# A hybrid encoder layer on one core: negated maximum inside the score pass, value halves read from PSUM, and four moves of work between queues

## The chip, the cores and the metric

The kernel runs on one core of a Trainium2 chip. The metric is the device time of one execution in microseconds (us). A core has five engines with an instruction queue each: TensorE (PE; its weight loads are listed apart as PEld), VectorE (DVE), ScalarE (ACT), GpSimd (POOL) and SyncE (SP, which only issues DMAs). DMAs are issued from SP's or GpSimd's queue. Each queue runs in order; an instruction that waits holds up all that stand behind it on its engine.

## The reference

One layer of an encoder over 4096 positions of width 1024, all in float32. A normed input goes through one wide projection, whose columns feed two groups. Group A is a bidirectional mLSTM with a chunkwise scan (32 chunks of 128, 4 heads of 128). Group B is windowed attention: 8 query heads on 2 key heads of 64, a window of 128 to either side, a relative-position bias and a sink logit per head. The outputs of both go through one output projection, the residual is added and a last norm taken. The part that the change touches most:

```python
scores = jnp.where(mask[None, :, None, None], scores + bias, NEG_INF)
sink_l = sink.astype(jnp.float32).reshape(B_KV_HEADS, Q_PER_KV)[:, :, None]
m = jnp.maximum(jnp.max(scores, axis=-1), sink_l)
p = jnp.exp(scores - m[..., None])
denom = jnp.sum(p, axis=-1) + jnp.exp(sink_l - m)
out = jnp.einsum('bnhgqk,bnkhd->bnqhgd', p, vw) / denom.transpose(0, 1, 4, 2, 3)[..., None]
```

## The kernel before

float32 products are made of three passes of a shorter format: each operand is split into a high half (a cast, on ACT) and a low half (the difference, on DVE), and high·low, low·high and high·high are added up in PSUM. So nearly every result of TensorE is followed by a pair: a cast on ACT and a subtraction on DVE behind it. PE's order is written out by hand: the program walks lists of "pieces" (work with dependencies) and spreads them over a list of "fill" (projection matmuls), and PE runs in exactly that order. The orders on the other engines are set by a scheduler, which takes what is ready, earlier work of the program first; `tc.high_priority` moves a group ahead, and `behind(c, x)` keeps a group from being issued ahead of the instruction x.

There are four stages, by the times of the profile: attention (0 to 607 us), projections of group A with its chunk sums (607 to 1205), the scan (1205 to 1700), and the output side (1700 to the end).

**Attention.** A slot `sl` is one block n of 128 queries and one key head (kv = sl % 2); there are 64. For each of a slot's four groups g (two heads by two halves of the queries), `att_a` multiplies queries with up to 320 keys into a PSUM tile `sp`; L383, one pass of DVE, adds the bias table G and writes s to SBUF, and its accumulator takes the row maximum into a column of `st`. After the fourth group L390 makes NG = min(−maximum, −sink) for all four columns at once, and four exps (L392, ACT) of s + NG follow. `att_t` transposes the exps in three groups of four (`tp`, PSUM tag "b", two buffers), L414 casts them and L415 makes the low half, which frees the buffer. `att_o` multiplies with the values into `op` (PSUM tag "c", one buffer); L438 and L439 (`ab`) read it out. `slot` mixes scores of slot sl + 2, transposes of sl and products of sl − 1. In between run the projections of later blocks: queries (`qp`; L559 and L563 split them), keys (`kk`, L496 to L502) and values (`vp`), and `norm_rows`, which squares two rows of blocks on ACT (L213, 1024 columns each). In steady state two blocks of queries (four slots) make a period of some 35 us. The values: L523 copies the second half of `vp` to `vg`, L524 adds the first, L527 casts and L528 subtracts, the last two from `vg` in SBUF. At the stage's end `sinks` adds the sinks' share, and `rnorm` (L800) takes the reciprocal of all denominators R, which is transposed and stored later.

**Projections.** Blocks of 512 positions from b = 7 down to 0. For each of 8 row groups m, matmuls with `xb` (loaded by L868 on SP; block 7's comes from the attention) give U; L1051 to L1058 apply the convolution and the activation, and L1060 stores the result to `q_d` (m < 4) or `k_d`. `weigh(n)` forms the weighted values of a chunk (`wvr` L1112, `wvh` L1114, `wvl` L1115); `ktp` transposes the keys (L1099), and L1101 and L1102 split them into `kt`; `kvp` multiplies the two into a state `kv`.

**Scan.** For a chunk n, `load` brings E (decay rows, 2 × 256 KB), W, q, k, v and others; GpSimd masks E (L1442), ACT takes its exponentials (L1446), DVE multiplies with the scores S (L1456), and `heads` uses the result. `pieces` of a chunk are spread over its share of the output side's matmuls (`P`, with operands `op` from L1239).

The call that orders a chunk of the scan, since the change turns on it:

```python
with behind(c, c.rawd if n == 0 else None):
    load(n + 2, ("e",))
    if n == 0:
        load(2, ("q",))
```

Of the kernel before, what the change touches and what calls it, by code (L numbers as in the profile page):

```python
# [9 lines left out]
F32 = mybir.dt.float32  # L10
# [3 lines left out]
ALU = mybir.AluOpType  # L14
# [14 lines left out]
def f32(ap):  # L29
    return ap.bitcast(F32)  # L30
# [85 lines left out]
def behind(c, ins):  # L116
    return c.tc.issue_after(ins.ins) if ins is not None else ExitStack()
# [43 lines left out]
def pass1(c):  # L161
    nc, tc, A = c.nc, c.tc, c.A
    NB = 16
    with ExitStack() as es:
# [196 lines left out]
        def att_a(sl, g):  # L361
# [10 lines left out]
            if g == 0:  # L372
                st = wk.tile([128, 4], F32, tag="st", bufs=4, name=f"st{sl}")
                ST[sl] = ([], list(range(jl // 128, jr // 128)), st)
            ps, _, mx = ST[sl]
            ng, rs = c.NG[:, kv, n, :], c.R[:, n, kv, :]
            sp = c.ps("a", [128, 384], f"sp{sl}_{g}")
            qt = qb[kv * 2 + m][:, qc // 64 + half].rearrange("p z q -> p (z q)")
            for z in range(2):
# [4 lines left out]
                                           in1=bias[0][:, kv * 2 + m, lo - 64 * half:hi - 64 * half],  # L384
                                           op0=ALU.add, op1=ALU.max, scale=1.0, scalar=-3e38,
                                           accum_out=mx[:, g:g + 1])
            ps.append(s)
            if g < 3:
                return
            nc.vector.scalar_tensor_tensor(ng, mx, -1.0, nsink[:, kv].rearrange("p h m -> p (h m)"), ALU.mult, ALU.min)  # L390
            for g in range(4):
                LAST["act"] = nc.scalar.activation(ps[g][:, kept(g)], ps[g][:, kept(g)], AF.Exp, bias=ng[:, g:g + 1],  # L392
                                                   accum_out=rs[:, g:g + 1])
# [11 lines left out]
        def att_t(sl, i):  # L405
            ps, js, _ = ST[sl]
            if i >= len(js):
# [98 lines left out]
        def vproj(b):  # L506
            R = {}

            def unit(i, k):
# [12 lines left out]
                with tc.high_priority(offset=EV):  # L522
                    nc.scalar.copy(vg, vp[:, 1, :])  # L523
                    nc.vector.tensor_add(vg, vp[:, 0, :], vg)  # L524
                vt = wk.tile([128, 2, 128], F32R, tag="v", bufs=7, name=f"v{n}")
                vv = vg[:, 0:128].rearrange("p (a d) -> p a d", a=2)
                nc.scalar.copy(vt[:, :, 0:64], vv)  # L527
                nc.vector.tensor_sub(vt[:, :, 64:128], vv, f32(vt[:, :, 0:64]))  # L528
                V[n] = vt
# [153 lines left out]
        fill = qproj(NB - 2) + kproj(NB - 1) + vproj(NB - 1) + qproj(NB - 1) + v2_units(range(31, 27, -1))  # L683
        interleave(fill, pieces)
        sinks()

# [111 lines left out]
def rnorm(c):  # L798
    nc = c.nc
    nc.vector.reciprocal(c.R, c.R)  # L800
    tp = c.ps("b", [128, 2, 128], "rtp")
# [76 lines left out]
def pass2(c):  # L878
    nc, tc, A = c.nc, c.tc, c.A
    with ExitStack() as es:  # L880
# [138 lines left out]
        def qkproj(b, m):  # L1019
# [6 lines left out]
            def unit(lo, hi, k, j):  # L1026
# [28 lines left out]
                def finish():  # L1055
# [3 lines left out]
                    dst = c.k_d if m >= 4 else c.q_d  # L1059
                    nc.sync.dma_start(dst[4 * b:4 * b + 4, :, h * 128:h * 128 + 128].rearrange("n p t -> p n t"),  # L1060
                                      acc.rearrange("p (n t) -> p n t", n=4))
# [83 lines left out]
        for b in range(7, -1, -1):  # L1145
# [40 lines left out]
            def kvp(n, hh):  # L1186
                if hh == 0 and n > n3 - 3:
                    weigh(n - 1)
                kvmm(n, hh)
# [226 lines left out]
def pass3(c):  # L1416
    nc, tc, A = c.nc, c.tc, c.A
    with ExitStack() as es:
# [9 lines left out]
        def load(n, names):  # L1428
            load_scan(c, n, names)
# [111 lines left out]
        for n in range(NCH):  # L1541
# [3 lines left out]
            if m < NCH:  # L1545
                with behind(c, c.em):
                    state(n)
            with behind(c, c.rawd if n == 0 else None):
                load(n + 2, ("e",))
                if n == 0:  # L1550
                    load(2, ("q",))
            fill = take(c, 42)
# [8 lines left out]
            pieces += [(lambda h=h: heads(n, h)) for h in range(NH)]  # L1561
            pieces.insert(4, lambda: load(m, ("v",)) if n else None)
            pieces.append(lambda: (load(n + 2, ("kf",)), weigh_q(m) if m > 1 else None))
            if n:
# [360 lines left out]
```

## Time and profile before

| what | value |
|---|---|
| time, median of 3 runs | 2175.59 us (2173.66 to 2176.89) |
| the profiled execution | 2170.39 us, its span 2168.7 us |
| granted clock of TensorE in it | 0.999 |
| busy: PE, DVE, ACT, POOL | 2116.4, 1547.1, 1132.2, 704.2 us |
| DMA | 460.71 MB, 212 GB/s on average |

The rows of the profile name a line of the kernel (L383), an engine, an operation, and the tiles that it writes and reads (`s<-sp,G`). Times are us from the start of the span, and durations of single instructions in ns where the column says so. "Idle before, releaser" is the time that an engine stood still ahead of a group, and what ended it. SPq is SP's queue, on which a row is the issue of a DMA. PEclk of 1.0 is TensorE at full clock.

### The profile page before, as it was taken

How to read it: one execution, taken by the hardware profiler on the slowest of the kernel's cores; microseconds unless marked ns; L12 is line 12 of the kernel's file. 1: busy time of each engine (PE TensorE's matmuls, PEld its weight loads, DVE VectorE, ACT ScalarE, POOL GpSimd, SP SyncE). 2: the span in 40 equal slices, each digit the busy share in tenths (PEclk: the TensorE clock that was granted, in tenths of full speed). 3: DMA queues.
4: the chain of work that ended last, by engine and by line, in shares of the span. 5: the costliest groups of instructions: out<-in, count | busy, mean ns of one | idle time of the engine just before them, and what ended most of it. 6: DMA issues, size and time to landing. Idle time of an engine off the chain costs nothing. (4 is left out here: it accounts for less than half of the span.)

```text
span 2168.7 us, 35317 instructions
## 1 busy us (share of the span) xinstructions
PE 2116.4 (98%) x12034; PEld 1834.4 (85%) x12034; DVE 1547.1 (71%) x3259; ACT 1132.2 (52%) x2764; POOL 704.2 (32%) x1049
## 2 busy tenths in 40 slices
PE   8999999999999999999999999999999999999998
PEld 7999999999887887888887888888888788888886
DVE  6777777878876786667566777777777443777776
ACT  7778777778654444444433455555555321323323
POOL 3575666653014234322310322223222111112222
PEclk9999999999999999999999999999999999999999
DMA  8563544433228556743676988888888998667775
GB/s 269 181 208 135 194 142 187 161 139 113 64 91 263 188 170 217 246 159 112 216 223 239 340 272 273 254 265 278 268 273 290 353 359 279 181 178 187 192 196 144
DMA packets 286432, 460.71 MB, mean 212 GB/s; under 512 B 23851, under 2 KB 151851, under 8 KB 284716
## 3 DMA queue, kind: packets, MB, share of 16 engines
q1 hardware_dynamic: 246880, 323.94, 46.5%
q0 software_dynamic: 39136, 134.25, 19.0%
q8 instruction: 95, 1.56, 0.3%
q14 instruction: 85, 0.70, 0.1%
q10 hardware_dynamic: 236, 0.27, 0.0%
HBM read 305.20 MB, written 153.17 MB: 211 GB/s over the span
## 5 line engine op out<-in xcount | busy, mean ns | idle before, releaser
L1342 PE MATMUL P<-wt,op 128*128 128x512 f32 x1344 | 360.4, 406 | 0.4 <-DMA op<-xT_d 0.4
L1034 PE MATMUL up<-xb,w 128*128 128x512 f32 x1344 | 335.0, 396 | 0.0
L1691 PE MATMUL o<-wo,yo 128*128 128x512 f32 (+1 forms) x1356 | 311.7, 392 | 0.0
L1691 PEld LDWEIGHTS o<-wo,yo 128*128 128x128 f32 x1356 | 253.2, 188 | 58.6
L1034 PEld LDWEIGHTS up<-xb,w 128*128 128x128 f32 x1344 | 245.1, 188 | 49.1
L1342 PEld LDWEIGHTS P<-wt,op 128*128 128x128 f32 x1344 | 238.5, 189 | 42.5 <-DMA op<-xT_d 0.8
L1053 DVE SCALAR_TENSOR_TENSOR qk<-U,cw,qk 128x512 f32<-128x512 f32 x256 | 194.0, 760 | 85.2 <-ACT qk L1051 81.7
L549 PE MATMUL qp<-xT,wqb 128*128 128x256 f32 x1536 | 241.5, 287 | 0.1
L549 PEld LDWEIGHTS qp<-xT,wqb 128*128 128x128 f32 x1536 | 213.2, 189 | 8.6 <-DVE wqb L320 0.5
L392 ACT ACTIVATE s<-s,NG 128x320 f32<-128x320 f32 (+1 forms) x256 | 140.2, 550 | 46.9 <-DVE NG L390 46.3
L1007 PE MATMUL v2p<-w,xb 128*128 128x512 f32 x672 | 159.1, 396 | 4.7 <-DMA xb<-xT_d 3.1
L1007 PEld LDWEIGHTS v2p<-w,xb 128*128 128x128 f32 x672 | 125.7, 188 | 36.8 <-DMA xb<-xT_d 4.0
L415 DVE TENSOR_TENSOR pt<-tp,pt 128x512 fp32r<-128x512 f32 x188 | 127.9, 687 | 34.1 <-ACT pt L414 32.8
L383 DVE CUSTOM_DVE_ANT_0 s<-sp,G 128x320 f32<-128x320 f32 (+1 forms) x256 | 122.3, 478 | 27.8 <-PE sp L380 25.8
L414 ACT CAST pt<-tp 128x512 fp32r<-128x512 f32 x188 | 108.6, 585 | 52.0 <-PE tp L412 40.3
L412 PE MATMUL tp<-ident,s 128*128 128x128 f32 x752 | 113.5, 273 | 15.9 <-DVE pt L415 15.6
L426 PE MATMUL op<-pt,v 128*128 128x512 f32 x376 | 120.5, 401 | 7.0 <-DVE ab L439 7.0
L380 PE MATMUL sp<-kk,q 128*128 128x320 f32 (+2 forms) x512 | 118.6, 312 | 1.3 <-DVE kk L502 0.8
L1493 ACT ACTIVATE hs<-num,r 128x128 f32<-128x128 f32 x128 | 46.7, 365 | 129.7 <-DVE r L1490 70.9
L151 PE MATMUL zbp<-xc,w 128*128 128x512 f32 x256 | 102.2, 399 | 1.9 <-DVE az L1405 1.4
L412 PEld LDWEIGHTS tp<-ident,s 128*128 128x128 f32 x752 | 85.5, 140 | 20.8 <-issue 17.7
L153 PE MATMUL zbp<-xc,w 128*128 128x512 f32 x256 | 101.0, 395 | 0.0
(307 smaller groups left out, 4543.2 us busy)
## 6 DMA issues: line engine op xcount, KB each, us to landing
xc<-xT_d SPq DMA_DIRECT2D x64, 512.0 KB, 7.3
xT_d<-xT POOLq DMA_DIRECT2D x52, 512.0 KB, 7.3
xb<-xT_d SPq DMA_DIRECT2D x48, 514.0 KB, 7.1
op<-xT_d SPq DMA_DIRECT2D x96, 256.0 KB, 5.5
E<-m_d SPq DMA_DIRECT2D x64, 256.0 KB, 4.3
W<-w_d SPq DMA_DIRECT2D x64, 256.0 KB, 5.9
y<-y_d SPq DMA_DIRECT2D x32, 512.0 KB, 3.4
out<-xr POOLq DMA_DIRECT2D x31, 512.0 KB, 4.4
```

The lines of the kernel that those rows point to most:

```text
L380: nc.tensor.matmul(sp[:, lo:hi], qt, kk[:, kv, z, col - 128 + lo:col - 128 + hi], start=(z == 0), stop=(z == 1))
L383: nc.vector.tensor_tensor_reduce(out=s[:, lo:hi], in0=sp[:, lo:hi], in1=bias[0][:, kv * 2 + m, lo - 64 * half:hi - 64 * half], op0=ALU.add ...
L392: LAST["act"] = nc.scalar.activation(ps[g][:, kept(g)], ps[g][:, kept(g)], AF.Exp, bias=ng[:, g:g + 1], accum_out=rs[:, g:g + 1])
L412: nc.tensor.transpose(tp[:, g * 128:(g + 1) * 128], ps[g][:, j * 128:(j + 1) * 128], c.ident)
L415: nc.vector.tensor_sub(pt[:, 1, :], tp, f32(pt[:, 0, :]))
L426: nc.tensor.matmul(op, vt, pt[:, z, :], start=(i == 0 and z == 0), stop=(i == len(js) - 1 and z == 1))
L549: nc.tensor.matmul(qp, wq[k // 2][:, k % 2, w, m * 128:m * 128 + 128], x[k], start=(k == 0 and j == 0), stop=(k == KT - 1 and j == 2))
L1007: nc.tensor.matmul(vp, a, wv[k // 2][:, k % 2, m, :], start=(k == 0 and j == 0), stop=(k == KT - 1 and j == 2))
L1034: nc.tensor.matmul(up[:, 0:hi - lo], w[k // 2][:, k % 2, a, cs], x, start=(k == 0 and j == 0), stop=(k == KT - 1 and j == 2))
L1053: nc.vector.scalar_tensor_tensor(acc, U[:, t:t + 512], cw[:, cm, t:t + 1], acc, ALU.mult, ALU.add)
L1342: nc.tensor.matmul(P[i], OPS[j, i][:, k, z, :], c.wt[i][k][m], start=k == 0 and a == 0, stop=k == 3 and a == 2)
L1691: nc.tensor.matmul(p, a[:, z, k, :], w[k // 2][:, k % 2, m, lo:hi], start=k == 0 and z == 1, stop=k == 3 and z == 0 and m == 0)
```

## The change

- L383 computes −(score + bias) and takes the minimum, starting from −sink, which it reads from a column of SBUF (`nsink`); the result goes to NG itself. L390 and the tile `st` are gone. s is stored negated, and the exps have a scale of −1.
- The sum of the two halves of `vp` is made by two adds, one of 128 columns (for b > 2 in place in PSUM) and one of 16 columns (to `vg`, the gates). For b > 2 the cast and the subtraction read the sum from PSUM, and stand in a high-priority group.
- The reciprocal in `rnorm` is issued behind the last L439 of the attention.
- The stores of `q_d` of block 7 are issued from GpSimd's queue in place of SP's.
- At block 0 of the projections the last three `weigh` are issued behind the `kt` pair that was last written by then.
- In the scan, E for chunk n + 2 is loaded as a piece of its own behind the first group of heads, instead of at the chunk's start (for n > 0), so that most chunks have 12 pieces where there were 11.

```diff
-                st = wk.tile([128, 4], F32, tag="st", bufs=4, name=f"st{sl}")
-                ST[sl] = ([], list(range(jl // 128, jr // 128)), st)
-            ps, _, mx = ST[sl]
+                ST[sl] = ([], list(range(jl // 128, jr // 128)))
+            ps, _ = ST[sl]
...
-                                           op0=ALU.add, op1=ALU.max, scale=1.0, scalar=-3e38,
-                                           accum_out=mx[:, g:g + 1])
+                                           op0=ALU.add, op1=ALU.min, scale=-1.0,
+                                           scalar=nsink[:, kv, half, m:m + 1], accum_out=ng[:, g:g + 1])
...
-            nc.vector.scalar_tensor_tensor(ng, mx, -1.0, nsink[:, kv].rearrange("p h m -> p (h m)"), ALU.mult, ALU.min)
             for g in range(4):
-                LAST["act"] = nc.scalar.activation(ps[g][:, kept(g)], ps[g][:, kept(g)], AF.Exp, bias=ng[:, g:g + 1],
+                LAST["act"] = nc.scalar.activation(ps[g][:, kept(g)], ps[g][:, kept(g)], AF.Exp, scale=-1.0, bias=ng[:, g:g + 1],
...
-                    nc.vector.tensor_add(vg, vp[:, 0, :], vg)
+                    for o, cs in ((vp[:, 0, 0:128] if b > 2 else vg[:, 0:128], slice(0, 128)), (vg[:, 128:144], slice(128, 144))):
+                        nc.vector.tensor_add(o, vp[:, 0, cs], vg[:, cs])
                 vt = wk.tile([128, 2, 128], F32R, tag="v", bufs=7, name=f"v{n}")
-                vv = vg[:, 0:128].rearrange("p (a d) -> p a d", a=2)
-                nc.scalar.copy(vt[:, :, 0:64], vv)
-                nc.vector.tensor_sub(vt[:, :, 64:128], vv, f32(vt[:, :, 0:64]))
+                vv = (vp[:, 0, 0:128] if b > 2 else vg[:, 0:128]).rearrange("p (a d) -> p a d", a=2)
+                with tc.high_priority(offset=EV if b > 2 else 0):
+                    nc.scalar.copy(vt[:, :, 0:64], vv)
+                    nc.vector.tensor_sub(vt[:, :, 64:128], vv, f32(vt[:, :, 0:64]))
...
         interleave(fill, pieces)
+        c.abv = LAST["abv"]
         sinks()
...
-    nc.vector.reciprocal(c.R, c.R)
+    with behind(c, c.abv):
+        nc.vector.reciprocal(c.R, c.R)
...
-                    nc.sync.dma_start(dst[4 * b:4 * b + 4, :, h * 128:h * 128 + 128].rearrange("n p t -> p n t"),
+                    q = nc.gpsimd if b == 7 and m < 4 else nc.sync
+                    q.dma_start(dst[4 * b:4 * b + 4, :, h * 128:h * 128 + 128].rearrange("n p t -> p n t"),
...
-                    weigh(n - 1)
+                    with behind(c, None if b else c.kta), behind(c, None if b else c.ktv):
+                        weigh(n - 1)
...
-            with behind(c, c.rawd if n == 0 else None):
-                load(n + 2, ("e",))
-                if n == 0:
-                    load(2, ("q",))
+            if n == 0:
+                with behind(c, c.rawd):
+                    load(2, ("e", "q"))
...
+            if n:
+                pieces.insert(3, lambda: load(n + 2, ("e",)))
```

The change also moves instructions on ACT, DVE, GpSimd and SP, since the scheduler sets their order. In the rows below a name carries two numbers, the program's own and a running one; the changed kernel's lines are 2 to 4 numbers off.

ACT in a steady period, around the squares `jk8`, before. `s0_` and `s1_` are score tiles of which a slot uses two and two, `pt16_2` the third transposed group of slot 16, whose cast frees the buffer that a group of slot 17 takes:

```order
L414 CAST pt16_1_2655<-tp16_1_2650 128x512
L392 ACTIVATE s0_0_136,R_95<-s0_0_136,NG_160 128x320
L392 ACTIVATE s0_1_137,R_95<-s0_1_137,NG_160 128x320
L559 ACTIVATE q5_1_2712<-qp5_1_2647 64x4x64 x2
L392 ACTIVATE s1_0_142,R_95<-s1_0_142,NG_160 128x320
L392 ACTIVATE s1_1_143,R_95<-s1_1_143,NG_160 128x320
L213 ACTIVATE jk8_0_2698,ss8_2697<-xr8_2588 128x1024
L213 ACTIVATE jk8_1_2700,ss8_2697<-xr8_2588 128x1024
L414 CAST pt16_2_2690<-tp16_2_2685 128x512
```

The same place after the change:

```order
L390 ACTIVATE s1_0_142,R_95<-s1_0_142,NG_160 128x320
L436 COPY ab7_2522<-op15_2576 64x2x4x64
L412 CAST pt16_1_2630<-tp16_1_2625 128x512
L390 ACTIVATE s1_1_143,R_95<-s1_1_143,NG_160 128x320
L213 ACTIVATE jk8_0_2672,ss8_2671<-xr8_2564 128x1024
L213 ACTIVATE jk8_1_2674,ss8_2671<-xr8_2564 128x1024
L559 ACTIVATE q5_1_2686<-qp5_1_2622 64x4x64 x2
L390 ACTIVATE s0_2_138,R_95<-s0_2_138,NG_160 128x320
L412 CAST pt16_2_2664<-tp16_2_2659 128x512
```

Between the casts of `pt16_1` and `pt16_2` stood all four exps of a slot and two squares; now there stand the last exp of that slot, the squares, and the first exp of the next slot.

DVE at the end of the projections, before (`kt0_h` are the key halves of block 0's four heads, `wvr`/`wvl` the weighted values of chunks 1 and 0):

```order
L1115 TENSOR_TENSOR wvl1_13491<-wvr1_13492,wvh1_13490 128x1032
L1112 TENSOR_TENSOR wvr0_13545<-v2_0_13002,TM_8490 128x4x129
L1053 SCALAR_TENSOR_TENSOR qk0_7_13324<-U0_7_13296,cw_7445,qk0_7_13324 128x512
L1058 SCALAR_TENSOR_TENSOR qk0_6_13286<-th0_6_13330,qk0_6_13286 128x512
L1102 TENSOR_TENSOR kt0_0_1_13367<-ktp0_0_13361,kt0_0_0_13366 128x512
L1102 TENSOR_TENSOR kt0_1_1_13387<-ktp0_1_13381,kt0_1_0_13386 128x512
L1053 SCALAR_TENSOR_TENSOR qk0_7_13324<-U0_7_13296,cw_7445,qk0_7_13324 128x512
L1115 TENSOR_TENSOR wvl0_13544<-wvr0_13545,wvh0_13543 128x1032
```

The same place after the change:

```order
L1105 TENSOR_TENSOR kt0_0_1_13271<-ktp0_0_13265,kt0_0_0_13270 128x512
L1055 SCALAR_TENSOR_TENSOR qk0_7_13228<-U0_7_13200,cw_7358,qk0_7_13228 128x512 x2
L1105 TENSOR_TENSOR kt0_1_1_13291<-ktp0_1_13285,kt0_1_0_13290 128x512
L1327 TENSOR_TENSOR o1_13306<-P0_1_13280,o0_13278 128x512
L1060 SCALAR_TENSOR_TENSOR qk0_7_13228<-th0_7_13295,qk0_7_13228 128x512
L1105 TENSOR_TENSOR kt0_2_1_13319<-ktp0_2_13313,kt0_2_0_13318 128x512
L1115 TENSOR_TENSOR wvr2_13330<-v2_2_12844,TM_8394 128x4x129
L1140 SCALAR_TENSOR_TENSOR C3_13336<-C4_12716,decay_8208,kv3_0_13338 128x129
L1329 TENSOR_TENSOR z0_13346<-P0_2_13308,o1_13306 128x512
L1118 TENSOR_TENSOR wvl2_13329<-wvr2_13330,wvh2_13328 128x1032
```

The weighting of chunks 2, 1 and 0 stood ahead of the four `kt` copies or between them; that of chunk 2 now stands behind the third copy, and the other two further on.

SP at the first loads of `xb` for block 6, before:

```order
L807 DMA r_d_80<-rt_8338 128x128 x2
L1060 DMA k_d_75<-qk7_6_8279 128x4x128
L1060 DMA k_d_75<-qk7_7_8397 128x4x128
L1060 DMA q_d_74<-qk7_0_8484 128x4x128
L868 DMA xb6_0_8664<-xT_d_69 128x2x514
L868 DMA xb6_1_8666<-xT_d_69 128x2x514
```

The same place after the change:

```order
L809 DMA r_d_80<-rt_8242 128x128 x2
L1063 DMA k_d_75<-qk7_6_8183 128x4x128
L1063 DMA k_d_75<-qk7_7_8301 128x4x128
L870 DMA xb6_0_8568<-xT_d_69 128x2x514
L870 DMA xb6_1_8570<-xT_d_69 128x2x514
```

The store of the first q rows of block 7 no longer stands ahead of the loads; it is in GpSimd's queue.

More of the change, by code (lines that the diff above doesn't have):

```diff
@@ L405, in att_t @@
         def att_t(sl, i):
-            ps, js, _ = ST[sl]
+            ps, js = ST[sl]
             if i >= len(js):
```

## Prediction

> **What bounds the kernel now.** I read the page first: the busy shares, then the chain.
>
> ```profile
> span 2168.7 us, 35317 instructions
> PE 2116.4 (98%) x12034; PEld 1834.4 (85%) x12034; DVE 1547.1 (71%) x3259; ACT 1132.2 (52%) x2764; POOL 704.2 (32%) x1049
> ```
>
> TensorE is busy for 2116.4 of 2168.7 us. The change leaves its instructions and their order alone up to the scan, and their number everywhere, so what can be won is the 2168.7 − 2116.4 = 52.3 us in which it idles. The next view is therefore the waits of PE (engine and line, what it waited for: us in total, times, longest):
>
> ```profile
> PE tp L412 <- DVE pt L415: 15.6, 13, 1.8
> PE op L426 <- DVE ab L439: 7.0, 6, 2.4
> PE bps L337 <- POOL ohb L300: 6.5, 1, 6.5
> PE v2p L1007 <- DMA xb<-xT_d: 3.1, 2, 2.1
> PE ktp L1099 <- DVE kt L1102: 2.8, 2, 1.5
> ```
>
> The edits touch four of these five. The 6.5 us at the start (bias table) stay. Restricted to 110 to 560 us, the first row reads 14.3 us in 10 waits: one of about 1.4 us in each period of some 35 us, the attention's steady state. The fence has that row and the next, then the busy time of PE, PEld, DVE, ACT and POOL in one such period, and then one of the waits, by the timelines of ACT, DVE and PE (start, duration, and in brackets the idle time before it and what ended it):
>
> ```profile
> PE tp L412 <- DVE pt L415: 14.3, 10, 1.8
> PE op L426 <- DVE ab L439: 1.0, 2, 0.7
> ...
> 228.00:263.00 35.00, 33.59 (x256) 32.35 (x255) 27.04 (x70) 27.21 (x72) 21.86 (x29) 1.00 0.46 162
> ...
> 231.38 0.56 ACT L392 ACTIVATE s<-s,NG 128x320 f32<-128x320 f32 x1 [2.20 <-DVE NG L390]
> ...
> 232.48 0.75 ACT L559 ACTIVATE q<-qp 64x256 fp32r<-64x256 f32 x2
> ...
> 234.37 1.04 ACT L213 ACTIVATE jk<-xr 128x1024 bf16<-128x1024 f32 x1
> 235.41 1.04 ACT L213 ACTIVATE jk<-xr 128x1024 bf16<-128x1024 f32 x1
> 236.57 1.07 ACT L414 CAST pt<-tp 128x512 fp32r<-128x512 f32 x2
> ...
> 229.32 0.49 DVE L383 CUSTOM_DVE_ANT_0 s<-sp,G 128x320 f32<-128x320 f32 x1
> ...
> 230.34 1.00 DVE L390 SCALAR_TENSOR_TENSOR NG<-st,nsink 128x4 f32<-128x4 f32 x1
> ...
> 237.19 1.29 DVE L415 TENSOR_TENSOR pt<-tp,pt 128x512 fp32r<-128x512 f32 x2
> ...
> 238.03 0.63 PE L412 MATMUL tp<-ident,s 128*128 128x128 f32 x4 [1.41 <-DVE pt L415]
> ```
>
> Read backwards: the transposes at 238.03 need a PSUM buffer which L415 frees at 237.88; L415 needs the cast L414, which at 236.57 is the first thing on ACT after four exps, two query copies and two squares L213. All four exps waited until 231.38 for L390, the four-column bias instruction, and ACT stood idle for 2.20 us before them. PE would have been ready at 238.03 − 1.41 = 236.62.
>
> **The negated maximum (64 times L390 out).** The pass L383 now yields the negated, sink-limited maximum, so an exp waits for its own L383 and not for the fourth. These are the groups of DVE up to 660 us (count, busy us, mean ns) and, below them, single lines (ns minimum, median, maximum):
>
> ```profile
> L390 DVE SCALAR_TENSOR_TENSOR NG<-st,nsink 128x4 f32<-128x4 f32 x64 | 42.2, 659 | 1.0
> L528 DVE TENSOR_TENSOR v<-vg,v 128x128 fp32r<-128x128 f32 x32 | 21.1, 661 | 0.1
> L524 DVE TENSOR_TENSOR vg<-vp,vg 128x144 f32<-128x144 f32 x32 | 9.4, 298 | 0.0
> ...
> L390 DVE SCALAR_TENSOR_TENSOR NG<-st,nsink x64: 143/164/1839, 39.6 to 592.8; 128x4 f32<-128x4 f32 x64
> ...
> L383 DVE CUSTOM_DVE_ANT_0 s<-sp,G x256: 345/481/494, 35.6 to 589.5; 128x320 f32<-128x320 f32 x120, 128x192 f32<-128x192 f32 x4, 128x256 f32<-128x256 f32 x4
> ...
> L1494 DVE SCALAR_TENSOR_TENSOR hs<-num,r,hs x128: 339/350/354, 1223.4 to 1682.2; 128x128 f32<-128x128 f32 x128
> ```
>
> Removed: 42.2 us of DVE. Added: L383 takes its starting value from a column of SBUF. Nothing in the trace shows that form of it. The nearest is L1494, of 128 columns with a column as scalar: 350 ns median, against 298 for L524 of 144 columns without one, so some 60 ns more on each of 256, 15 us of DVE. From below I put 0, since the column might be fetched beside the start. I take 60 ns; DVE still comes out 27 us lighter.
>
> The new time of that cast, by rows: the last L383 of a slot ends at 229.32 + 0.49 + 0.08 (its accumulator) = 229.9; the last exp, now alone, takes 0.56 to 230.45; the squares, which the order puts right behind it, 2 × 1.04 to 232.5; two query copies 0.75 to 233.3; one exp of the next slot 0.56 to 233.9; the cast half of 1.07 and a little, to 234.5; L415 0.68, to 235.2. That is 1.4 us ahead of 236.62, so the wait goes. With 60 ns on three L383 it is 1.2 us ahead. What is late next is the output product op, which waits for ab (L439): its PSUM buffer is the only one of its kind, and its copy now stands behind a cast and an exp. From the 1.0 us in two waits that op has in the same window I allow 0.25 us a period. Gain: 14.3 − 10 × 0.25 = 11.8 us; bounds 14.3, and 0 if the order on ACT only passes the delay on.
>
> Outside the steady state, both smaller: of the 15.6 us of tp, 1.3 lie outside that window, ahead of it for the most part; I take a gain of 1.0 (0 to 1.3). Near 40 us, the order puts three exps ahead of the casts of the second key block that stood behind them: at most 3 × 0.56 us, and the exps there are narrower. I take a loss of 1.5 (0 to 1.7).
>
> **Value halves from PSUM.** L524 becomes two adds, 128 columns in place in PSUM and 16 to SBUF; L528 (and its cast) read PSUM for 26 of the 32 blocks. Added: 32 small adds of about 0.16 us (L390's median, 4 columns), 5 us. Removed: L528 at a mean of 661 ns becomes the like of L524, 298, which is 26 × 0.36 = 9 us. What lies behind the 661:
>
> ```profile
> L528 DVE TENSOR_TENSOR v<-vg,v x32: 273/292/2280, 23.7 to 543.0; 128x128 fp32r<-128x128 f32 x32
> ```
>
> A median of 292 and a maximum of 2280: it stretches where a GpSimd instruction runs beside it. L390 (164, maximum 1839) does the same. L524, L383 and L1494 never do; each of these has one operand in PSUM. [...] The PSUM buffer of the projection is held through two instructions more, about 0.6 us; there are three such buffers, and no wait of PE on them stands in the rows above. Net 0 for PE, apart from what is counted already.
>
> **Three edits at stage ends.** Rows from the timelines of DVE, SP and PE:
>
> ```profile
> 597.85 1.74 DVE L800 RECIPROCAL R<-R 128x256 f32<-128x256 f32 x1
> 599.62 0.69 DVE L439 TENSOR_TENSOR ab<-op,ab 64x512 f32<-64x512 f32 x1
> 600.37 0.73 PE L426 MATMUL op<-pt,v 128*128 128x512 f32 x2 [2.37 <-DVE ab L439]
> ...
> 647.60 1.01 PE L1034 MATMUL up<-xT,w 128*128 128x258 f32 x7
> ...
> 652.13 0.36 SPq L1060 DMA_DIRECT2D q_d<-qk  x1
> 652.72 7.88 SPq L868 DMA_DIRECT2D xb<-xT_d  x8
> 674.91 1.67 PE L1007 MATMUL v2p<-w,xb 128*128 128x512 f32 x6 [1.00 <-DMA xb<-xT_d]
> 678.68 0.50 PE L1007 MATMUL v2p<-w,xb 128*128 128x512 f32 x1 [2.10 <-DMA xb<-xT_d]
> ...
> 1194.57 1.22 DVE L1115 TENSOR_TENSOR wvl<-wvr,wvh 128x1032 fp32r<-128x1032 f32 x1
> 1193.54 0.63 PE L1099 MATMUL ktp<-ident,qk 128*128 128x128 f32 x4 [1.51 <-DVE kt L1102]
> 1198.50 0.65 PE L1099 MATMUL ktp<-ident,qk 128*128 128x128 f32 x4 [1.29 <-DVE kt L1102]
> ```
>
> (a) The reciprocal of 1.74 us stands ahead of an ab add that PE waits 2.37 us for. Moved behind the last ab add, it takes its 1.74 us with it: gain 1.7 (0 to 2.4). Its reader, the transposes in rnorm, comes more than 20 us later, in the projections.
>
> (b) SP issues the loads of xb for block 6 only once the store of q_d has had its operand, at 652.13. Four q stores go to GpSimd's queue, and the next thing to hold the first load is the release of the tile it lands in, which by the end of PE's matmuls from 647.60 I estimate at 648.6 at the earliest. So the loads run up to 3 us earlier; two landings were late by 1.0 and 2.1: gain 2.5 (0 to 3.1). The stores now stand in GpSimd's queue, and hold there what follows them until their operand is done; that queue carries memsets and shares of the weighting which PE needs several us later.
>
> (c) At the end of the projections the last three weightings (L1112, L1115) stood ahead of copies kt for which PE waited 1.51 and 1.29 us. They now stand behind the third and fourth kt. The products that need them begin some 3 us after that; two passes on DVE and one on ACT, 0.7 + 1.22 + 1.05, just fit. Gain 2.5 (−1 to 2.8).
>
> **The scan's E loads.** Issued after the first head group, about 4 us later than now. The rows in the middle of the scan:
>
> ```profile
> 1404.83 0.64 POOL L1442 TENSOR_SCALAR_AFFINE_SELECT E<-E 128x512 f32<-128x512 f32 x1 [5.42 <-DMA E<-m_d]
> 1409.66 2.43 ACT L1446 ACTIVATE E<-E,TM 128x128 f32<-128x128 f32 x8
> 1421.21 0.68 DVE L1456 TENSOR_TENSOR E<-S,E 128x512 f32<-128x512 f32 x1
> ```
>
> E is used at 1421.21, 9 us after the exps end; 4 us fit. GpSimd, waiting in order for E, delays the small power behind it (norm of the heads), which PE needs some 6 us later. I take 0, with bounds of −1 and +5, the latter if the sixteen chunks lose 0.3 us each.
>
> **Sum.** −11.8 − 1.0 + 1.5 − 1.7 − 2.5 − 2.5 = −18.0 us, of 52.3 idle. The profiled execution took 2170.39 us, 0.24% below the median of 2175.59; on the median the forecast is 2157.6, 0.8% less. Differences under 0.2% (4.4 us) are no more than a measurement of this kernel can tell from none. With the terms' bounds the main case reaches from about 2150 to 2164.
>
> **Rivals.** *A new wait takes half.* The ACT order now alternates exps and casts; if ab or the score buffers are late by 0.7 us a period, 7 of the 11.8 us come back, and with half of the stage ends about 9 us remain: 2166. For it speaks that ACT is 27.2 of 35 us busy in such a period and keeps its order; against it the 1.2 us of margin worked out above.
>
> *The change doesn't do what it says.* The squares still stand ahead of that cast. If the exp ahead of them waits for something else, say a late score, the wait stays, and the ends (−6.7, less what fails) with the loss at the start give −3: 2173.
>
> *Slower.* If the scalar column makes L383 stretch beside GpSimd as L390 does, by the same 0.5 us on average (659 − 164), each period of 16 passes gets 8 us more DVE against 8 us idle (27.0 of 35 busy) and 2.6 freed (four L390). In order and at PE's side, half of the 8 would show: 4 × 15 periods − 18 = +42 us, 2218. It turns the sign from about 0.15 us a pass, a mean of 0.63 for L383. L1494 speaks against it: a column and one SBUF operand, and no start of 128 above 354 ns.
>
> **How the numbers follow.** Main case 0.56, half 0.26, nothing 0.10, slower 0.08. Faster is main plus half, 0.82; the same 0.10; slower 0.08. The range takes main and half whole and the edge of the third: 2148 to 2172.
>
> **What would show it.** Right: in the waits of PE between 110 and 560 us, tp for L415's successor falls from 14.3 us to under 3, and ACT starts the squares less than 1 us after the slot's last L383; L383's mean stays under 0.56; ktp, v2p and op at 600 us lose their rows; PE's idle time falls to about 34 us with its busy time unchanged. Wrong: L383 with a maximum far above 0.5 us, a row of PE waiting for ab or for the key casts with over 8 us, or idle PE between 1205 and 1700 us.

## The result, and the profile after

The changed kernel took 2163.94 us (median of 4 runs, 2162.39 to 2164.78) against 2176.24 us (4 runs) of the kernel before on the same chip: a ratio of 0.9945, interval 0.9927 to 0.9962. That is 12.3 us, where 18.0 were forecast; the range held it. Two later batches on other chips gave 0.9932 (0.9910 to 0.9954) and 0.9956 (0.9941 to 0.9972). The page of the changed kernel:

```profile
span 2161.9 us, 35288 instructions
## 1 busy us (share of the span) xinstructions
PE 2121.2 (98%) x12034; PEld 1838.9 (85%) x12034; DVE 1524.7 (71%) x3227; ACT 1143.6 (53%) x2764; POOL 707.1 (33%) x1053
```

PE's idle time fell from 52.3 to 2161.9 − 2121.2 = 40.7 us, 11.6 less, but its busy time rose by 4.8, with as many matmuls; the span fell by 6.8. Part of these 4.8 us is TensorE's clock and part lies in the scan; both are taken up below. PE's waits of the whole span, and then those of 110 to 560 us:

```profile
PE op L424 <- DVE ab L437: 9.0, 9, 2.8
PE bps L337 <- POOL ohb L300: 6.4, 1, 6.4
PE kv L151 <- DVE C L1140: 2.6, 2, 1.8
PE P L1346 <- DVE o L1337: 1.7, 3, 0.7
PE xtp L460 <- DVE kk L500: 1.7, 1, 1.7
...
PE op L424 <- DVE ab L437: 5.5, 7, 1.9
PE sp L379 <- DVE kk L500: 1.0, 1, 1.0
```

Of the five rows shown before, tp, v2p and ktp have left the list, and the 2.37 us that op waited for at 600 us are 0.70. New are kv, P and xtp, and op is at the top: the output product waits for its only PSUM buffer. One steady period as shown before, by the timeline of ACT:

```profile
227.37 0.56 ACT L390 ACTIVATE s<-s,NG 128x320 f32<-128x320 f32 x1 [0.74 <-DVE NG L382]
...
227.93 1.04 ACT L213 ACTIVATE jk<-xr 128x1024 bf16<-128x1024 f32 x1
...
228.97 1.04 ACT L213 ACTIVATE jk<-xr 128x1024 bf16<-128x1024 f32 x1
...
230.01 0.76 ACT L559 ACTIVATE q<-qp 64x256 fp32r<-64x256 f32 x2
230.79 0.56 ACT L390 ACTIVATE s<-s,NG 128x320 f32<-128x320 f32 x1
...
231.47 0.59 ACT L412 CAST pt<-tp 128x512 fp32r<-128x512 f32 x1
```

One exp, the squares, two copies, one exp, the cast: the chain that the prediction wrote down, 4.1 us from the start of the exp to the start of the cast, against 4.0 there (229.9 to 233.9).

PE's order is the same in both kernels up to the scan, so the start of the same matmul can be taken from both traces. The difference (after less before) at some places, by the times of before:

| place | us | after less before |
|---|---|---|
| start of the attention | 40 | −0.1 |
| behind the second key block | 60 | +1.6 |
| start of the steady state | 110 | +0.9 |
| its end | 450 | −11.0 |
| | 470 | −7.5 |
| before, behind the reciprocal | 560, 605 | −6.5, −11.4 |
| before, behind the xb loads | 660, 690 | −7.8, −12.4 |
| before, behind the kt copies | 1190, 1203 | −12.9, −15.8 |
| first and last product of the scan | 1217.6, 1679.2 | −14.7, −7.8 |

The gains stand at the places where they were expected, though not each by the edit that it was put down to (below). They reach 15.8 us, after 3.5 us had been given back at 450 to 470 us and 3.6 between 605 and 660; the scan gives back 6.9 more.

### The profile page after: what moved, and what is told of

Same layout as the page of the kernel before. It is cut to its first block, busy times and chain, and to the rows that moved or that the text cites. A ratio compares the mean times of both kernels' runs of the same rounds, so it can differ in the third digit from the quotient of the medians.

```text
span 2161.9 us, 35288 instructions
## 1 busy us (share of the span) xinstructions
PE 2121.2 (98%) x12034; PEld 1838.9 (85%) x12034; DVE 1524.7 (71%) x3227; ACT 1143.6 (53%) x2764; POOL 707.1 (33%) x1053
## 4 chain that ended last, share of the span: by engine, by line
PE 85%; DMA 5%; DVE 5%; ACT 3%; issue 2%; POOL 0%; SPq 0%; POOLq 0%; ACTq 0%; DVEq 0%
PE up L1036 16%; PE o L1696 14%; PE P L1346 12%; PE qp L549 8%; PE v2p L1009 7%; PE op L424 4%; PE tp L410 3%; PE sp L379 3%; PE zbp L151 3%; PE zbp L152 3%; PE zbp L153 3%; PE num L1483 2%; PE num L1482 2%; PE vp L515 1%; DMA W<-w_d 1%
## 5 line engine op out<-in xcount | busy, mean ns | idle before, releaser
L1036 PE MATMUL up<-xb,w 128*128 128x512 f32 x1344 | 334.8, 396 | 0.0
L1036 PEld LDWEIGHTS up<-xb,w 128*128 128x128 f32 x1344 | 245.0, 188 | 48.9
L413 DVE TENSOR_TENSOR pt<-tp,pt 128x512 fp32r<-128x512 f32 x188 | 129.7, 690 | 81.2 <-ACT pt L412 77.5
L390 ACT ACTIVATE s<-s,NG 128x320 f32<-128x320 f32 (+1 forms) x256 | 142.4, 557 | 51.6 <-DVE NG L382 50.2
L382 DVE CUSTOM_DVE_ANT_0 s<-sp,G,nsink 128x320 f32<-128x320 f32 (+1 forms) x256 | 138.1, 540 | 38.9 <-PE sp L379 33.9
L151 PE MATMUL zbp<-xc,w 128*128 128x512 f32 x256 | 102.0, 398 | 1.8 <-DVE w L108 1.1
L152 PE MATMUL zbp<-xc,w 128*128 128x512 f32 x256 | 100.9, 394 | 0.0
L153 PE MATMUL zbp<-xc,w 128*128 128x512 f32 x256 | 100.9, 394 | 0.0
```

Of the source, the lines that this page charges most:

```text
L151: nc.tensor.matmul(out, wl, xh, start=first, stop=False)
L152: nc.tensor.matmul(out, wh, xl, start=False, stop=False)
L153: nc.tensor.matmul(out, wh, xh, start=False, stop=last)
L1036: nc.tensor.matmul(up[:, 0:hi - lo], w[k // 2][:, k % 2, a, cs], x, start=(k == 0 and j == 0), stop=(k == KT - 1 and j == 2))
```

## The experiments

Theory: the ten steady waits go by the negated maximum alone, the small edits win what stands behind them, and the late E costs the scan some 5 us through GpSimd. Rivals: the value halves make the gain; or what E's place costs is DMA or clock. Three batches ran on three chips, and the kernel before itself is at 2179.94, 2173.09 and 2179.07 us in them, so that times are compared only within a batch or as ratios.

**The negated maximum alone** (all else as before):

```diff
-                                           op0=ALU.add, op1=ALU.max, scale=1.0, scalar=-3e38,
-                                           accum_out=mx[:, g:g + 1])
+                                           op0=ALU.add, op1=ALU.min, scale=-1.0,
+                                           scalar=nsink[:, kv, half, m:m + 1], accum_out=ng[:, g:g + 1])
...
-            nc.vector.scalar_tensor_tensor(ng, mx, -1.0, nsink[:, kv].rearrange("p h m -> p (h m)"), ALU.mult, ALU.min)
...
+                LAST["act"] = nc.scalar.activation(ps[g][:, kept(g)], ps[g][:, kept(g)], AF.Exp, scale=-1.0, bias=ng[:, g:g + 1],
```

> The kernel before with the negated maximum alone (L390 gone, exps with a scale of -1); everything else as before. Theory: the ten steady waits of PE for the transposes' buffer (14.3 us) go, at the price of about 2 us at the start, where exps stand ahead of the second key block's casts: PE waits tp below 3 us in 110 to 560 us, time 9 to 12 us below before, the waits at 600, 675 and 1195 us and the scan as before. Rival: the value halves, which shorten DVE, make the gain; then tp keeps over 7 us here and the time falls by less than 4 us.

Measured: 2168.82 against 2179.94 us, ratio 0.9950 (0.9936 to 0.9964), 11 us. PE's waits in 110 to 560 us, and then two rows from the end of the attention:

```profile
PE op L424 <- DVE ab L437: 6.5, 10, 1.1
PE tp L410 <- DVE pt L413: 3.6, 1, 3.6
PE sp L379 <- DVE kk L500: 1.0, 1, 1.0
...
589.24 1.74 DVE L798 RECIPROCAL R<-R 128x256 f32<-128x256 f32 x1
...
593.65 0.73 PE L424 MATMUL op<-pt,v 128*128 128x512 f32 x2 [0.78 <-DVE ab L437]
```

The ten waits are gone; the one tp wait that is left is another (at 106 us a cast of x on ACT waited 5.0 us for a store to land). So this edit alone wins nearly the time of the whole change.

Two parts of the expectation failed. The wait at 600 us, which was to stay, fell from 2.37 to 0.78 us: with no edit to it, the reciprocal came earlier here, and no longer right ahead of the ab that PE waits for. And the scan, which was to stay too, took 466.7 us from the first to the last product num against 461.6 before; no run shows why. With that, the start, the wait of 3.6 us and a stretch of TensorE's clock at half speed behind it, the traced execution has a span only 0.8 us below that of before. The 11 us rest on the times; the trace shows which waits went.

**The value halves alone:**

```diff
-                    nc.vector.tensor_add(vg, vp[:, 0, :], vg)
+                    for o, cs in ((vp[:, 0, 0:128] if b > 2 else vg[:, 0:128], slice(0, 128)), (vg[:, 128:144], slice(128, 144))):
+                        nc.vector.tensor_add(o, vp[:, 0, cs], vg[:, cs])
...
+                vv = (vp[:, 0, 0:128] if b > 2 else vg[:, 0:128]).rearrange("p (a d) -> p a d", a=2)
```

> The kernel before with the value halves from PSUM alone. Theory: DVE loses the long L528 (mean 661 to about 290 ns), but the exps still wait for L390 and the squares stand where they stood: the ten waits stay (over 11 us in 110 to 560), time 0 to 3 us below before. Rival (these halves make the gain): the ten waits fall below 7 us, time 6 us or more below.

Measured: 2174.60 us, ratio 0.9981 (0.9971 to 0.9991): about 4 us, 2 to 6 by the interval, where 0 to 3 were expected. The waits of PE in 110 to 560 us, and two groups of DVE:

```profile
PE tp L412 <- DVE pt L415: 16.5, 10, 1.9
...
L390 DVE SCALAR_TENSOR_TENSOR NG<-st,nsink 128x4 f32<-128x4 f32 x64 | 45.1, 705 | 0.9
...
L530 DVE TENSOR_TENSOR v<-vp,v 128x128 fp32r<-128x128 f32 x26 | 7.2, 277 | 0.0
L530 DVE TENSOR_TENSOR v<-vg,v 128x128 fp32r<-128x128 f32 x6 | 3.7, 637 | 0.0
```

The subtraction that reads PSUM takes 277 ns, and at most 282; the six that still read two operands of SBUF take 637 on average, with a median of 285 and one of 2286. That was right. But all ten waits stand, since L390 is as long as ever, so the rival falls as the cause of the steady waits. What the 4 us are is not shown: at the first product of the scan this trace is 2.3 us behind the first one of before. Nor do the two edits' shares, 11 and 4 us, add up to the change's 12.

**E at the chunk's start again**, run twice:

```diff
+            with behind(c, c.rawd if n == 0 else None):
+                load(n + 2, ("e",))
+                if n == 0:
+                    load(2, ("q",))
-            if n == 0:
-                with behind(c, c.rawd):
-                    load(2, ("e", "q"))
...
-            if n:
-                pieces.insert(3, lambda: load(n + 2, ("e",)))
```

> The changed kernel with E loaded at a chunk's start again (11 pieces). Theory: in the changed kernel GpSimd waits for the later E ahead of the small power ss of the head norm, DVE's L1512 waits for that (25.5 us in 26 times against 4.3 in 5), and PE for DVE; this costs the 5.3 us that the changed kernel loses against before between 1200 and 1700 us. Then L1512's wait for POOL falls below 8 us, PE's waits in the scan go back to those of before, and the time is 4 to 6 us below the changed kernel. Rival (the scan's loss is of the DMA queues or the granted clock, not of E's place): within 1.5 us of the changed kernel.

Measured: 2167.59 us, ratio 0.9950 (0.9935 to 0.9965): no better than the changed kernel's ratio on another chip, and that is why both were run again side by side:

> The changed kernel, unaltered, beside the next three on one chip, since a difference of a few us between kernels cannot be read across chips. Expected 0.993 to 0.995 of before; in the scan DVE's L1512 waits over 20 us in all for GpSimd.

> The changed kernel with E loaded at a chunk's start (as in the earlier run of this edit, now beside the changed kernel). Theory: the late E costs PE 4 to 6 us in the scan; the time is 3 to 6 us below the changed kernel of this batch, the scan's length (first to last num) is that of before within 2 us, and the attention differs only by chance. Rival: what the scan gains here is lost to the clock or to the DMAs elsewhere; within 1.5 us.

Measured: 2169.87 us for the changed kernel, 2170.16 us with E back. In time the theory failed. The profile with E back had four half-speed stretches of TensorE's clock (next section but one) against two, and its scan took 467.5 us (first to last product num), only 0.9 less than the changed kernel's beside it. Over all traces the scan is shorter with the early E: six traces with the late E lie at 467.7 to 469.6 us, seven with the early E and 11 pieces at 461.6, 461.7, 462.1, 462.9, 463.3, 466.7 and 467.5, mean 463.7, 4.8 less. But the two stretches do not hold the same work: with 12 pieces three more matmuls (zbp, 0.44, 0.39 and 0.39 us on average) stand ahead of the last num, 2701 against 2698, so that some 3.6 us are left for E's edit. The windows of the scan before, after and in the last run below (us, PE, PEld, DVE, ACT and POOL busy, granted clock, DMA share, GB/s):

```profile
1217.55:1679.15 461.60, 460.55 (x2698) 399.12 (x2697) 345.49 (x893) 257.01 (x792) 128.08 (x151) 1.00 0.86 277
...
1202.85:1671.32 468.47, 464.05 (x2701) 400.48 (x2700) 350.49 (x894) 258.28 (x793) 129.66 (x152) 1.00 0.87 273
...
1204.99:1667.05 462.06, 460.32 (x2698) 399.20 (x2697) 346.29 (x893) 256.92 (x793) 132.16 (x151) 1.00 0.86 277
```

Of the 6.9 us between the first two rows, 3.5 are PE's busy time, at a granted clock of 1.00 (1.2 of them the three matmuls), and 3.4 are idle time. PE's waits for DVE's o L1337, which reads out a product P, come in all six traces with the late E (0.7 to 2.0 us) and in none of the eight others.

The mechanism was tried with E at the chunk's start and an empty piece in its place:

```diff
             if n:
-                pieces.insert(3, lambda: load(n + 2, ("e",)))
+                pieces.insert(3, lambda: None)
```

> E loaded at the chunk's start, but an empty piece kept in its place, so that the 12 pieces fall on the matmuls as in the changed kernel. It tells the place of the load from the shift of the pieces. Theory (the late load): scan as with E back, L1512 waits for GpSimd under 8 us. Rival (the shift of the pieces): scan as in the changed kernel, 4 to 6 us longer.

Measured: 2164.59 us (ratio 0.9940, 0.9918 to 0.9961), a scan of 464.0 us. The waits of DVE for GpSimd's power in the scan, of the changed kernel and then of this one:

```profile
DVE hs L1512 <- POOL ss L1508: 22.3, 23, 1.5
...
DVE hs L1512 <- POOL ss L1508: 16.5, 14, 1.2
```

Most of these waits stay, so they come with the twelfth piece more than with the late load; and the scan is as short with them as the average of the early E. The chain from GpSimd to PE is refuted as the main cause. That the late load itself costs is what this single trace says (464.0 against 468.4 of the changed kernel beside it, with the same 12 pieces), but one run with the early load had 467.5 too, so the way by which it costs stays open.

**Block 7's q stores on SP again, and on ACT's queue:**

```diff
-                    q = nc.gpsimd if b == 7 and m < 4 else nc.sync
+                    q = nc.sync            # the first; the second: nc.scalar if b == 7 and m < 4 else nc.sync
```

> The changed kernel with block 7's q stores on SP's queue again. Theory: the two waits for xb near 675 us come back (4.3 us by the step in PE's start times), and the new wait of PE for the states kv at 652 us (1.8 us) goes with the cause, so that the kernel is 2 to 3 us slower than the changed one. Rival: the kv wait has nothing to do with the stores; it stays, and the kernel is over 4 us slower.

> The changed kernel with block 7's q stores on ACT's queue in place of GpSimd's. It separates the two sides of that edit: the loads of xb go early as in the changed kernel, but GpSimd's queue no longer carries the stores. Theory A (the stores hold up GpSimd's queue or its kf and cb stores): the wait of PE for kv near 650 us (1.8 us) is gone, with the xb waits still gone. Theory B (the earlier xb loads crowd the DMA engines, and the kf store that ACT waits for lands late): the kv wait is still there, over 1 us.

Measured: 2170.34 us with SP, ratio 0.9959 (0.9947 to 0.9972); 2162.22 us for the one run with ACT's queue. These times decide nothing: the first has no changed kernel beside it, and its interval overlaps all three of the changed kernel; the second is one run. PE's waits between 640 and 690 us: changed kernel, SP, ACT:

```profile
PE kv L151 <- DVE C L1140: 1.8, 1, 1.8
...
PE v2p L1009 <- DMA xb<-xT_d: 1.7, 1, 1.7
PE v2p L1009 <- ACT U L1040: 0.7, 1, 0.7
...
PE kv L151 <- DVE C L1140: 1.1, 1, 1.1
```

With SP the xb wait is back and kv gone; on ACT's queue kv is smaller and still there (0.8 us in the last run below). So GpSimd's queue is at most a part of the kv wait. The rest, by the chain in the changed kernel's trace: ACT's copy kf waits for the store of the previous kf to land, and the cast wvh, DVE's wvl and the update C stand behind it; PE needs the buffer that C frees.

```profile
648.67 0.27 ACT L1138 COPY kf<-kv 128x129 f32<-128x129 f32 x1 [3.51 <-DMA kf_d<-kf]
648.83 1.06 ACT L1117 CAST wvh<-wvr 128x1032 fp32r<-128x1032 f32 x1
...
652.00 0.36 PE L151 MATMUL kv<-wvh,kt 128*128 128x258 f32 x1 [1.77 <-DVE C L1140]
```

The xb loads now run beside that store. That they are what makes it late is the likely reading, not a shown one. For it speaks that in the kernel before, the kf store issued at 651.24 us, 1.5 us ahead of the first of these loads, lands after 3.1 us, and the three that are issued beside them after 7.1 to 7.7; the one that ACT waits for here was issued at 641.38 and landed some 7.3 us later.

**No column** (a constant as starting value, which leaves the sink out of the maximum):

```diff
-                                           scalar=nsink[:, kv, half, m:m + 1], accum_out=ng[:, g:g + 1])
+                                           scalar=3e38, accum_out=ng[:, g:g + 1])
```

> The changed kernel with a constant as L382's starting value in place of the column of -sink: the maximum is no longer limited by the sink, so this leaves the sink out of the bias. It prices the column. Measured so far: L382 takes 546 ns on average with it, 484 ns without it before. Theory: the 62 ns come from the column (484 ns here again), 15.9 us of DVE in all; PE feels them only where DVE is late, in the waits op on ab (5.5 us in 110 to 560 us in the changed kernel), which fall by 1 to 3 us: 0 to 3 us faster than the changed kernel. Rival: the 62 ns come from the other operation (minimum, negative scale); L382 stays at 546 ns and the time as it is.

Measured: L382 at a median of 491 ns against 543 in the changed kernel, so the column costs 52 ns; the time is 2164.26 us against 2160.87 of the changed kernel in that batch, not less (intervals overlap). The op waits in 110 to 560 us fell to 2.9 from 3.8 us, and one wait of 5.2 us for a value cast came up elsewhere. So 13 us less of DVE's time (256 × 52 ns) brought no gain that these runs can tell.

**Both kernels again**, for second profiles:

> The changed kernel again, with nothing altered, on the chip of this batch. It tells what of the differences between traces belongs to the kernel and what to one execution. Theory (the clock decides part of the spread): TensorE's clock falls to one half for 3.41 us after a window of 3.41 us in which PE was busy for less than about 0.47; the changed kernel has some three such windows at most, with single waits of 2 us or more at the start, near 450 us or near 650 us. Then the waits op on ab near 450 us and kv near 650 us are there again, the scan loses again at L1337's buffer (about 2 us in three waits), and each half-speed stretch stands right behind a window with less than 0.48. Rival: the half-speed stretches fall anywhere.

> The kernel before again, for a second profile. Its first profiled execution had no half-speed stretch ahead of its end and took 2170.39 us, below all of its timed runs. Theory: an ordinary execution of it has one to three such stretches, each costing about 1.7 us directly, behind one of the ten waits of about 1.4 us where such a wait falls whole into a window; expected 2174 to 2183 us, the ten waits as before. Rival: the first profile was as good as any; no stretch, within 2 us of 2170.

Measured: 2160.87 against 2173.09 us. Of before's ten tp waits the second profile shows ten again (14.4 us), and its time was 2170.30 us, not the 2174 to 2183 that the theory named: the rival's time, though with one half-speed stretch. The changed kernel's waits at op, kv, P and xtp were there again. Its one half-speed stretch stands behind a window with PE busy for 0.25, as expected, but lasts for two windows, the first of them 0.65 busy.

**E back, and the q stores on ACT's queue:**

> The same with block 7's q stores on ACT's queue. The wait for kv near 650 us was 1.1 us with that, 1.7 with GpSimd's queue. Expected 0 to 2 us below the run with E at the chunk's start, the best of the four; rival: ACT's time for the issues (four, ahead of exps of no one) shows nowhere, and the two are equal.

Measured: 2164.52 us, 5.6 less than the run with E back, where 0 to 2 were expected, and 5.4 less than the changed kernel beside it; ratio to before 0.9931 (0.9914 to 0.9949) against 0.9956 (0.9941 to 0.9972). The intervals just overlap. It is the best of that batch beside the 2164.59 of the empty piece. PE's wait for kv near 650 us is 0.8 us here against 1.9 with E back alone; what the rest is, no run shows.

## Why the prediction was right, and where it was off

- **The steady waits** (11.8 forecast). Right in mechanism and nearly in size: tp's 14.3 us went to none, op rose from 1.0 to 5.5 us in 7 waits (3.8 in the second profile), where 2.5 were allowed. By the table 11.9 us between 110 and 450. The step that failed is the even 0.25 us a period: up to 440 us op has one wait over 0.6 us (0.75), and then 1.87 us at once, at 452. There DVE had stood idle for 2.67 us, until 449.47, and then had two L382 and an L413 to do ahead of ab (L437):

```profile
449.47 0.55 DVE L382 CUSTOM_DVE_ANT_0 s<-sp,G,nsink 128x320 f32<-128x320 f32 x1 [2.67 <-PE kp L483]
...
451.13 0.69 DVE L437 TENSOR_TENSOR ab<-op,ab 64x512 f32<-64x512 f32 x1
...
451.88 0.50 PE L424 MATMUL op<-pt,v 128*128 128x512 f32 x1 [1.87 <-DVE ab L437]
```

In this trace it is the order on DVE, and not its load, that op pays for.

- **The scalar column** (60 ns): 62 ns on the mean of the widest form (546 against 484), of which the experiment puts 52 (median) on the column itself; maximum 554, and 553 among the 115 of 256 that ran beside a computing instruction of GpSimd, so L382 does not stretch there and the slower rival is out.
- **The start** (loss of 1.5): +1.6 at 60 us, as the row xtp <- kk says. **60 to 110** (gain of 1.0): the small waits went, but op waited 2.8 us once, for ab, whose copy waited 3.56 us for the store of the previous ab to land; net 0.7 gained. In the two other profiles of the changed kernel that wait was 3.7 and 3.8 us, the clock fell to one half as well, and between 60 and 110 us 2.8 and 1.8 us were lost; so that the term has the right sign in the first profile is luck.
- **Value halves** (0 for PE): 277 to 283 ns where 298 were taken; in the run of this edit alone the steady waits stayed, and yet its time was some 4 us lower, which the 0 does not hold.
- **The reciprocal** (1.7): op's wait went from 2.37 to 0.70 us, 1.7, but the number is right by luck. With the negated maximum alone, and the reciprocal free to run as before, that wait was 0.78 us, so that moving it is worth some 0.1 us behind the other edit. The whole step from 560 to 605 us is 4.9 us here and 4.8 there.
- **xb** (2.5): the two waits went (4.6 us by the table from 660 to 690, with a small one for ACT), and kv, whose wait of 1.8 us lies ahead of 660, took part of it back. Net 2.6 by PE's starts at 640 and 690 us (−9.8 and −12.4), but the prediction's last sentence on this edit was wrong in its kind: what came late was no memset or weighting in GpSimd's queue, but a store's landing.
- **kt** (2.5): ktp's 2.8 us went, and kv took back 0.8; by the table 1.8 us are left at the first product of the scan (−12.9 to −14.7).
- **E** (0, bounds −1 and +5): the mis-sized term. The scan was 6.9 us longer than before in the first pair, 4.8 on average over the traces, and 5.7 and 3.6 without the three matmuls that have changed sides. Idle PE in the scan, which the prediction named as a sign of being wrong, rose from 1.1 to 4.4 us, while PE's idle time fell to 40.7 us and not to 34.
- **Not in the sum at all:** the clock, next section. The first rival, "a new wait takes half", named 2166, and what came lies between it and the main case, nearer to the rival, though not at the place that it named alone: op, kv, the scan and the clock share it. (The rival's own terms, 11.8 − 7 + 1.0 − 1.5 + 3.35, give 7.7 us and not 9, so 2168.)

The first two profiled pairs show 6.8 and 5.7 us, the medians 12.3 at first, and 12.2 and 9.2 in the second and third batch. The executions of before that were profiled, 2170.39 and 2170.30 us, are among its fastest of all (2169.33 to 2184.97); the rest were not traced. So about half of the gain that the medians show is not accounted for by a trace. The granted clock explains some of the spread: in the first batch of experiments seven runs of before at 0.996 took 2181.6 us on average, seven at 0.997 2179.4, three at 0.998 2175.8. It does not explain the gain: at a clock of 0.997 in both kernels, the changed one is 15.3 us faster in the second batch (two runs each) and 8.3 in the third (three against four). What makes most executions of before slower than the two that were traced stays open.

## What the runs showed of the hardware

Part of PE's 4.8 us of added busy time is half-speed stretches. In each trace the clock is 1.00 or, for single stretches, 0.50; the first 20 us and what lies behind PE's last matmul aside, 24 of these last 3.41 us and three 6.83. The first trace of the changed kernel has two of 3.41, and the first of before none. By the granted clock they lose 3.41 × 0.5 = 1.7 us each, which is an estimate: in the second, at 616.70 us, L1036's matmuls of 258 columns start every 214 ns (median), elsewhere in the trace every 120. So by that estimate the clock takes 3.4 us, the scan adds 3.5 at full clock (above), and smaller differences of the other sign make up the rest. Three pairs of windows, each the 3.41 us ahead of such a stretch and the stretch itself (columns as above, PEclk third from the end), and a fourth pair in which nothing happened:

```profile
449.45:452.86 3.41, 1.54 (x10) 1.27 (x9) 3.01 (x7) 3.17 (x9) 3.41 (x4) 1.00 0.93 314
452.86:456.28 3.42, 3.42 (x15) 3.23 (x15) 2.74 (x7) 2.16 (x7) 2.72 (x4) 0.50 0.67 228
...
113.09:116.50 3.41, 0.02 (x1) 0.02 (x1) 2.46 (x6) 2.77 (x9) 1.93 (x4) 1.00 0.97 171
116.50:119.91 3.41, 3.41 (x15) 3.41 (x16) 2.91 (x9) 2.73 (x8) 2.44 (x6) 0.50 0.99 394
...
656.04:659.45 3.41, 1.57 (x14) 1.45 (x13) 1.92 (x5) 0.00 (x0) 0.90 (x2) 1.00 1.02 312
659.45:662.86 3.41, 3.41 (x19) 3.41 (x18) 0.96 (x3) 0.70 (x3) 0.18 (x1) 0.50 1.02 370
...
448.57:451.98 3.41, 1.63 (x14) 1.43 (x12) 1.45 (x7) 3.37 (x8) 1.11 (x2) 1.00 0.00 0
451.98:455.40 3.42, 3.33 (x27) 3.28 (x27) 3.17 (x7) 1.54 (x3) 1.26 (x3) 1.00 0.39 154
```

PE was busy for 1.54, 0.02 and 1.57 us of the window in the first three (changed kernel; negated maximum alone; E back), and for 1.63 in the fourth (value halves alone), after which the clock stayed. Within a trace the stretches lie whole multiples of 3.41 us apart (452.86 and 616.70 us in the changed kernel, 48 of them), so the windows stand on a grid. The kernel does not set where it lies: in its two traces, the one kernel with E back has stretches at 659.45 and at 657.84 us, 1.61 us apart. Of the 27 stretches in the 14 traces, 21 follow a window with PE busy for 0.46 of it or less, and every such window at full speed has one behind it. No window at full speed with more than 0.47 did this, but for one kind: six times a window that began at 612 to 626 us, 0.92 busy, with the eight matmuls of one column in it (L817 of the changed kernel), was followed by a stretch, and in other traces not; why is open. Within the three long stretches the bound is another: their first windows, at half speed themselves, were busy for 0.22, 0.65 and 0.76, and a second one at half speed followed each.

In the first pair 45% of busy time did not keep the clock up (1.54 of 3.41 us). What halves it, no run shows; that the idle time of the window ahead is the cause is the author's reading of these rows.

By that reading a wait has two prices. Ten waits of 1.4 us, one in each period, cost what they last, because a window that holds one whole is still 0.56 busy or more in before's first trace. The margin is thin: in its second trace one such window is 0.48 busy. One wait of 1.9 us can cost some 1.7 us more, by the estimate above, if by chance of the grid it lies whole in one window, as op's 1.87 us up to 451.88 us did. The change took away the first kind and left some of the second: op near 80 and 450 us, kv near 650 us.

## What to carry to other kernels

Where one engine is the bound and its order is fixed, take the same instruction's start in both traces and subtract: the steps of that difference show each gain and each loss at its place, which a total hides. Remove the instruction that makes several others wait together, before making any of them shorter: 64 small instructions out were worth 11 us, a faster subtraction some 4, and the waits that it was to end stayed. Where edits stand together, run the largest of them alone: here it took the gain that another had been given. When short waits are gone, look for the longest that is left; in these traces, 1.84 us of idle time (3.41 − 1.57) or more in one window at full speed was also followed by half speed, 1.78 (3.41 − 1.63) was not.
